# Order and engine of the state-space table preparation in a two-layer decoder trunk (GLA, then S5)

## The chip, the cores and the metric

The kernel runs on one core of one Trainium2 chip. The metric is the device time of one execution in microseconds (us), lower is better. The core's engines run their own instruction streams and wait for each other by semaphores: TensorE (PE; PEld is its weight loading), VectorE (DVE), ScalarE (ACT), GpSimd (POOL), and SyncE (SP), which here only issues DMAs. ACT and POOL issue DMAs too. An engine takes its instructions in order: one that waits holds up all behind it.

## What is computed

Two residual layers on x (512 tokens, 1024 wide), then an RMSNorm. Layer 0 is gated linear attention (4 heads, keys 128, values 512 wide), layer 1 a diagonal state-space layer (S5) with 128 groups of 16 channels and 64 complex states each. Cut to what matters:

```
x = x + gla(rmsnorm(x))                 # q,k,v,z,r = h @ w_in; o * silu(z) @ w_out
h = rmsnorm(x);  u, z = split(h @ w_in)
dt = exp(log_dt);  lam_bar = exp(lam * dt)        # complex, per group and state
b_coef = (lam_bar - 1) / lam;  b_bar = b_coef * b
states[t] = lam_bar * states[t-1] + b_bar @ u[t]
y = real(states @ c) + d_skip * u
y = gelu(y);  y = y * sigmoid(y @ w_glu + b_glu) * silu(z)
x = x + y @ w_out
```

## The kernel before

Matmul operands are split into a high and a low fp32r part, and each product is three matmuls (`three`). Weights come in units of 512 KB: SP loads a raw tile (`wraw`, two buffers, L175), ScalarE makes the high part (`whl`, L180 or L158), and the low part is made either by VectorE (L159) or by ScalarE writing the negated raw tile (L181) to which a POOL DMA adds the weights again (L182).

The S5 layer is computed in chunks of T = 8 tokens from tables that depend only on the parameters, not on x. These tables are made during the GLA layer, in the gaps of its engines. `S5Prep.small` is a generator that makes the small per-state values. Its steps are called by `tick()`: first loads, then step sizes, angles and `bcr`, `bci` (b_coef); then on POOL the powers PR, PI of lam_bar (`cmul` on POOL, with scratch tiles `ta`, `tb`) and the angle products `et` (L1139 to L1147); then the scaled `bcr`, `bci`, the scale `em2` and, by a matmul, `kap`; from these LR, LI (powers times b_coef) and `pc`, `pd` (powers times kap), all on POOL; then the stores of these values to HBM by SP (`r8d`, `kdd`, `etd`, `bcd`, 16 stores to `lpt`, 4 to `pw`), LR and LI after a transposition on TensorE; then the loads of BA, BB, rho8h and kd, where ScalarE negates half of BB (L1236). `zero()` clears the left part of the convolution buffer `kz` by 16 stores of SP.

The heavy part is a plan of steps, `prep.step(mark, code, cb)`, one for each of 16 blocks of 8 groups: F (`compute` on VectorE, `load` of the next block, storing the block before), Z (`finish_z`: convolution matrix, diagonal), E (`etab`: a table of angles from `et`), G (`gcopy`). `hook()` takes the next step from the plan after a fixed number of matmul units, from the second head of the GLA layer on. Each head runs gate, `proj_qk`, `proj_v`, the output projection of the head before, and `proj_z`, with the attention pieces (scores, state, mix) woven in. The output of a head is transposed (L399) and split (L161, L162) before its projection.

The final order on each engine is not the program's: a list scheduler simulates the engines and issues by priority, which is program order plus an offset (`later(n)`). `issue_after(ins)` keeps what is inside behind `ins` on its engine; `mark` holds the last matmul, split and weight load. Tiles come from pools of fixed size; a tile used again waits for its readers.

The scale table `etac` (16 by 8 values from `etd`) is read much later, by `uscale` in the S5 layer (L744), but its load stands on ScalarE's queue at L692 without a mark.

Of the kernel before, what the change touches and what calls it, by code (L numbers as in the profile page):

```python
# [87 lines left out]
def trunk_kernel(  # L88
# [539 lines left out]
    for h in range(NH):  # L628
# [26 lines left out]
        if h == 0:  # L655
            weave([z], tk)
            prep.zero()
            tick()
# [33 lines left out]
    A.dma_start(out=etac, in_=bass.AP(prep.etd.tensor, prep.etd.offset, [[0, 16], [NB, GB], [1, NB]]))  # L692
# [237 lines left out]
class S5Prep:  # L930
    def __init__(self, tc, dr, C_, T_, PT, ident, q4, q2, big, tmp, s_bi, s_xc):
# [12 lines left out]
        self.bcd = dr.tile([2, NS, NG], F32, name="bcd")  # L944
# [7 lines left out]
    def zero(self):  # L952
        zero = self.tmp()[:, :112]
        self.nc.gpsimd.memset(zero, 0.0)
        kzf = self.kz.bitcast(F32).rearrange("g i w -> (g i) w")
        for k in range(16):
            self.nc.sync.dma_start(out=kzf[k * P:(k + 1) * P, 0:112], in_=zero)
# [4 lines left out]
    def small(self, lam_re, lam_im, log_dt, s_d):  # L962
# [157 lines left out]
        def cmul(dr_, di_, xr, xi, yr, yi, wv):  # L1120
            u, v = ta[:, :, :wv], tb[:, :, :wv]
            tt(u, xr, yr, MUL)
            tt(v, xi, yi, MUL)
            tt(dr_, u, v, SUB)
            tt(u, xr, yi, MUL)
            tt(v, xi, yr, MUL)
            tt(di_, u, v, ADD)
# [11 lines left out]
        self.et = [self.big().rearrange("p (g c) -> p g c", c=8) for _ in range(4)]  # L1139
        for er, ei, k0 in ((self.et[2], self.et[3], 1), (self.et[0], self.et[1], 4)):  # L1140
            G.memset(er[:, :, 0:1], 1.0)
            G.memset(ei[:, :, 0:1], 0.0)
            for k in range(3):
                wv = 2 ** k
                cb_ = cosv[:, k0 + k, :].unsqueeze(2).to_broadcast([P, W, wv])
                sb_ = sinv[:, k0 + k, :].unsqueeze(2).to_broadcast([P, W, wv])
                cmul(er[:, :, wv:2 * wv], ei[:, :, wv:2 * wv], er[:, :, :wv], ei[:, :, :wv], cb_, sb_, wv)  # L1147
        dm = self.dm = C_([P, 16], "dm")
        G.tensor_copy(out=dm, in_=self.ident[:, 0:16])
        for g in range(1, GB):  # L1150
            tt(dm, dm, self.ident[:, 16 * g:16 * g + 16], ADD)
        self.par = C_([P, 2], "par")
        V.tensor_reduce(out=self.par, in_=self.ident.rearrange("p (q e i) -> p e q i", e=2, i=16), axis=AX.XY, op=ALU.add)
        V.tensor_scalar(out=self.par, in0=self.par, scalar1=2.0 ** -SS, scalar2=None, op0=MUL)
# [14 lines left out]
        vt(bci, bci, bet, MUL)  # L1169
        vt(t1, cmx, eb, MUL)  # L1170
# [21 lines left out]
             bcr.unsqueeze(2).to_broadcast([P, W, 8]), bci.unsqueeze(2).to_broadcast([P, W, 8]), 8)  # L1192
# [3 lines left out]
        tt(pc[:, :, 0, :], PR[:, :, 0:8], kb, MUL)  # L1196
        tt(pd[:, :, 1, :], PI[:, :, 0:8], kb, MUL)
        ts(pc[:, :, 1, :], pd[:, :, 1, :], -1.0, MUL)
        ts(pd[:, :, 0, :], pc[:, :, 0, :], -1.0, MUL)
        G.tensor_copy(out=pd[:, :, 1, :], in_=pc[:, :, 1, :])  # L1200
# [8 lines left out]
        for ri, b in enumerate((bcr, bci)):  # L1209
            for k in range(2):  # L1210
                nc.sync.dma_start(out=self.bcd[ri][:, k * 64:(k + 1) * 64], in_=b[k * 64:(k + 1) * 64, :])
        for ri, src in enumerate((LR, LI)):
            for q in range(2):
                pt = self.PT()
                for k in range(4):
                    PE.transpose(pt[:64, k * P:(k + 1) * P], src[:, :, 4 * q + k], self.ident)
                ev = h2k()[:64].rearrange("g (a b c) -> g a b c", a=4, b=2)
                V.tensor_copy(out=ev.rearrange("g a b c -> g (a b c)"), in_=pt[:64, :])
                for k in range(4):
                    jp = 7 - (4 * q + k)  # L1220
                    nc.sync.dma_start(out=self.lpt[jp, :, ri].rearrange("(q g) p -> g q p", q=2), in_=ev[:, k])
        for ri, src in enumerate((pc, pd)):
            for k in range(2):
                nc.sync.dma_start(out=self.pw[ri * 64:(ri + 1) * 64, k * 64:(k + 1) * 64, :].rearrange("p g t -> p (g t)"),
                                  in_=src[k * 64:(k + 1) * 64].rearrange("p g k t -> p (g k t)"))
# [193 lines left out]
```

## Time and profile before

| | us |
|---|---|
| median of 3 runs | 1041.02 (1040.5 to 1044.96) |
| profiled execution, its own time | 1047.47 |
| its span in the trace | 1045.8 |
| PE busy / share | 918.1 / 88% |
| DVE busy / share | 714.4 / 68% |
| ACT busy / share | 471.8 / 45% |
| POOL busy / share | 141.8 / 14% |

Busy shares are averages over stages with different limits. Matmuls overlap in the trace, so the pace of a stretch is read from its matmul count. "Idle before" in a timeline is the time for which the engine stood ahead of an instruction, and the name behind the arrow is what released it. The granted clock is a share of full speed.

### The profile page before, as it was taken

How to read it: one execution, taken by the hardware profiler on the slowest of the kernel's cores; microseconds unless marked ns; L12 is line 12 of the kernel's file. 1: busy time of each engine (PE TensorE's matmuls, PEld its weight loads, DVE VectorE, ACT ScalarE, POOL GpSimd, SP SyncE). 2: the span in 40 equal slices, each digit the busy share in tenths (PEclk: the TensorE clock that was granted, in tenths of full speed). 3: DMA queues.
4: the chain of work that ended last, by engine and by line, in shares of the span. 5: the costliest groups of instructions: out<-in, count | busy, mean ns of one | idle time of the engine just before them, and what ended most of it. 6: DMA issues, size and time to landing. Idle time of an engine off the chain costs nothing.

```text
span 1045.8 us, 13633 instructions
## 1 busy us (share of the span) xinstructions
PE 918.1 (88%) x5019; PEld 716.4 (69%) x5019; DVE 714.4 (68%) x1225; ACT 471.8 (45%) x707; POOL 141.8 (14%) x248
## 2 busy tenths in 40 slices
PE   6795961799979983989998979999999999999996
PEld 5573740576757762757777768787778888888885
DVE  5793459996998688887947758798998542324322
ACT  5553342554635554533666573743443532313212
POOL 3174701131112221110310000000000000000000
PEclk9997985899979996999999989999989999999998
DMA  8884466899979999798676436788756422353312
GB/s 259 230 182 93 86 188 179 250 306 276 285 225 242 287 296 288 193 306 287 228 237 186 153 100 221 243 274 256 230 155 215 132 95 86 101 161 101 101 61 80
DMA packets 116915, 205.78 MB, mean 197 GB/s; under 512 B 32401, under 2 KB 67777, under 8 KB 116849
## 3 DMA queue, kind: packets, MB, share of 16 engines
q1 hardware_dynamic: 100736, 154.68, 48.2%
q0 software_dynamic: 13152, 45.24, 16.5%
q10 hardware_dynamic: 2960, 4.99, 1.4%
q8 instruction: 39, 0.64, 0.3%
q14 instruction: 28, 0.22, 0.1%
HBM read 167.69 MB, written 45.59 MB: 204 GB/s over the span
## 4 chain that ended last, share of the span: by engine, by line
PE 55%; DMA 13%; DVE 12%; issue 9%; ACT 6%; SPq 2%; POOL 1%; ACTq 0%; POOLq 0%; DVEq 0%
PE pd L193 7%; PE pd L194 7%; PE pd L195 6%; PE pd L190 5%; PE pd L189 5%; PE pd L191 5%; ACT u L723 3%; DMA big<-s_xc 3%; DMA wraw<-w_v 2%; PE po L189 2%; PE po L190 2%; PE po L191 2%; DMA q<-s_bi 2%; PE pt L189 1%; PE pt L190 1%
## 5 line engine op out<-in xcount | busy, mean ns | idle before, releaser
L159 DVE TENSOR_TENSOR whl<-wraw,whl 128x1024 fp32r<-128x1024 f32 x100 | 122.2, 1224 | 162.9 <-ACT whl L158 161.1
L158 ACT CAST whl<-wraw 128x1024 fp32r<-128x1024 f32 x100 | 104.9, 1049 | 200.8 <-PE pd L194 59.7
L193 PE MATMUL pd<-whl,actA 128*128 128x512 f32 x384 | 153.5, 405 | 15.6 <-ACT whl L158 9.6
L194 PE MATMUL pd<-whl,actA 128*128 128x512 f32 x384 | 153.9, 401 | 0.0
L195 PE MATMUL pd<-whl,actA 128*128 128x512 f32 x384 | 151.9, 401 | 0.0
L189 PE MATMUL pd<-actA,whl 128*128 128x512 f32 x256 | 102.9, 409 | 8.8 <-ACT u L723 7.4
L191 PE MATMUL pd<-actA,whl 128*128 128x512 f32 x256 | 102.4, 401 | 0.0
L193 PEld LDWEIGHTS pd<-whl,actA 128*128 128x128 f32 x384 | 73.7, 192 | 33.6 <-ACT whl L158 9.6
L195 PEld LDWEIGHTS pd<-whl,actA 128*128 128x128 f32 x384 | 73.3, 191 | 17.7 <-issue 2.4
L194 PEld LDWEIGHTS pd<-whl,actA 128*128 128x128 f32 x384 | 73.5, 191 | 16.2 <-issue 0.8
L193 PE MATMUL pd<-whl,q 128*128 128x512 f32 x192 | 78.8, 411 | 5.2 <-DVE tmp L387 4.9
L194 PE MATMUL pd<-whl,q 128*128 128x512 f32 x192 | 78.4, 408 | 0.0
L189 PEld LDWEIGHTS pd<-actA,whl 128*128 128x128 f32 x256 | 49.2, 192 | 21.3 <-ACT u L723 8.3
L180 ACT CAST whl<-wraw 128x1024 fp32r<-128x1024 f32 x36 | 37.7, 1047 | 57.0 <-PE pd L194 31.6
L191 PEld LDWEIGHTS pd<-actA,whl 128*128 128x128 f32 x256 | 49.1, 192 | 11.4
L189 PE MATMUL po<-actA,whl 128*128 128x512 f32 x128 | 51.4, 402 | 3.0 <-ACT whl L180 3.0
L190 PE MATMUL pd<-actA,whl 128*128 128x512 f32 x128 | 52.0, 406 | 0.0
L191 PE MATMUL po<-actA,whl 128*128 128x512 f32 x128 | 50.3, 395 | 1.5 <-DMA whl<-w_qk 1.5
L195 PE MATMUL pd<-whl,q 128*128 128x512 f32 x128 | 51.5, 412 | 0.0
L723 ACT ACTIVATE u<-pd,rsP 64x256 f32<-64x256 f32 x64 | 47.9, 748 | 3.1 <-DVE rsP L690 2.2
L190 PE MATMUL pd<-big,whl 128*128 128x512 f32 x120 | 48.6, 407 | 0.6 <-DVE big L159 0.6
L193 PEld LDWEIGHTS pd<-whl,q 128*128 128x128 f32 x192 | 37.4, 195 | 16.2 <-DVE tmp L387 5.3
(331 smaller groups left out, 2035.6 us busy)
## 6 DMA issues: line engine op xcount, KB each, us to landing
wraw<-w_glu SPq DMA_DIRECT2D x32, 512.0 KB, 3.5
wraw<-w_v SPq DMA_DIRECT2D x16, 512.0 KB, 4.5
wraw<-w_z SPq DMA_DIRECT2D x16, 512.0 KB, 5.8
whl<-w_z POOLq DMA_DIRECT2D x16, 512.0 KB, 9.2
q<-lpt SPq DMA_DIRECT2D x16, 512.0 KB, 5.7
q<-s_bi SPq DMA_DIRECT2D x16, 512.0 KB, 7.6
wraw<-w_out SPq DMA_DIRECT2D x16, 512.0 KB, 7.7
bmd<-q POOLq DMA_DIRECT2D x16, 512.0 KB, 6.9
```

Of the source, the lines that this page charges most:

```text
L158: i0 = A.copy(out=dst_hi, in_=src)
L159: i1 = V.tensor_tensor(out=dst_lo, in0=src, in1=f(dst_hi), op=SUB)
L180: A.copy(out=hi, in_=raw)
L189: PE.matmul(acc, lhsT=wh, rhs=ah, start=first, stop=False)
L190: PE.matmul(acc, lhsT=wh, rhs=al, start=False, stop=False)
L191: mark["pe"] = PE.matmul(acc, lhsT=wl, rhs=ah, start=False, stop=last).ins
L193: PE.matmul(acc, lhsT=ah, rhs=wh, start=first, stop=False)
L194: PE.matmul(acc, lhsT=ah, rhs=wl, start=False, stop=False)
L195: mark["pe"] = PE.matmul(acc, lhsT=al, rhs=wh, start=False, stop=last).ins
L723: A.activation(out=dst, in_=src, func=AF.Copy, scale=rsP[hs, tb:tb + 1])
```

## The change

Seven edits. (1) `bcd` holds a third table, the negated `bci`, and the lower half of BB is loaded from it; ScalarE's negation is gone. (2) LR, LI, `pc` go from POOL to VectorE, `pd` to ScalarE, and the angle products `et` (still on POOL) and `dm`, `par` are made after the stores in the program. (3) The 16 stores to `lpt` become 4, the transposes being taken in reverse order. (4) The load of `etac` is issued by SP, behind the weight load last marked. (5) `zero()` is one POOL store instead of 16 SP stores. (6) The first block's load is a step "L" of its own, between the last `tick()` of the first head and `zero()`; the F step of block 0 no longer issues it. (7) The diagonal is added by one instruction instead of two.

```diff
         if h == 0:
             weave([z], tk)
+            tick()
+            prep.step(mark, "L", 0)
             prep.zero()
-            tick()
...
-    A.dma_start(out=etac, in_=bass.AP(prep.etd.tensor, prep.etd.offset, [[0, 16], [NB, GB], [1, NB]]))
+    with tc.issue_after(mark["sp"]):
+        S.dma_start(out=etac, in_=bass.AP(prep.etd.tensor, prep.etd.offset, [[0, 16], [NB, GB], [1, NB]]))
...
-        kzf = self.kz.bitcast(F32).rearrange("g i w -> (g i) w")
-        for k in range(16):
-            self.nc.sync.dma_start(out=kzf[k * P:(k + 1) * P, 0:112], in_=zero)
+        kzf = self.kz.bitcast(F32).rearrange("g i w -> (g i) w").rearrange("(k p) w -> p k w", p=P)
+        self.nc.gpsimd.dma_start(out=kzf[:, :, 0:112], in_=zero.unsqueeze(1).to_broadcast([P, 16, 112]))
...
-        def cmul(dr_, di_, xr, xi, yr, yi, wv):
+        def cmul(dr_, di_, xr, xi, yr, yi, wv, E=G):
...
-        self.et = [self.big().rearrange("p (g c) -> p g c", c=8) for _ in range(4)]
...   (the whole block L1139 to L1154, et, dm, par, moves behind the stores)
+        nbi = t64()
+        vs(nbi, bci, -1.0, MUL)
...
         cmul(LR, LI, PR[:, :, 1:9], PI[:, :, 1:9],
-             bcr.unsqueeze(2).to_broadcast([P, W, 8]), bci.unsqueeze(2).to_broadcast([P, W, 8]), 8)
+             bcr.unsqueeze(2).to_broadcast([P, W, 8]), bci.unsqueeze(2).to_broadcast([P, W, 8]), 8, V)
...
-        tt(pc[:, :, 0, :], PR[:, :, 0:8], kb, MUL)
-        tt(pd[:, :, 1, :], PI[:, :, 0:8], kb, MUL)
-        ts(pc[:, :, 1, :], pd[:, :, 1, :], -1.0, MUL)
-        ts(pd[:, :, 0, :], pc[:, :, 0, :], -1.0, MUL)
-        G.tensor_copy(out=pd[:, :, 1, :], in_=pc[:, :, 1, :])
+        vt(pc[:, :, 0, :], PR[:, :, 0:8], kb, MUL)
+        stt(pc[:, :, 1, :], PI[:, :, 0:8], -1.0, kb, MUL, MUL)
+        A.activation(out=pd[:, :, 0, :], in_=pc[:, :, 0, :], func=AF.Copy, scale=-1.0)
+        A.copy(out=pd[:, :, 1, :], in_=pc[:, :, 1, :])
...
-        for ri, b in enumerate((bcr, bci)):
+        for ri, b in enumerate((bcr, bci, nbi)):
...
-                for k in range(4):
-                    jp = 7 - (4 * q + k)
-                    nc.sync.dma_start(out=self.lpt[jp, :, ri].rearrange("(q g) p -> g q p", q=2), in_=ev[:, k])
+                nc.sync.dma_start(out=self.lpt[4 - 4 * q:8 - 4 * q, :, ri].rearrange("j (q g) p -> g j q p", q=2), in_=ev)
...
-            nc.sync.dma_start(out=self.BB[hs], in_=self.bcd[1])
+            nc.sync.dma_start(out=self.BB[hs], in_=self.bcd[2 - k])
...
-        A.activation(out=self.BB[0:64], in_=self.BB[0:64], func=AF.Copy, scale=-1.0)
...
-        dk = self.C2([P, 16], "dk")
-        V.tensor_tensor(out=dk, in0=self.dm, in1=self.kd[:, cb:cb + 1].to_broadcast([P, 16]), op=MUL)
-        V.tensor_tensor(out=ke[:, 0:16], in0=ke[:, 0:16], in1=dk, op=ADD)
+        V.scalar_tensor_tensor(out=ke[:, 0:16], in0=self.dm, scalar=self.kd[:, cb:cb + 1], in1=ke[:, 0:16],
+                               op0=MUL, op1=ADD)
...
-                else:
-                    self.load(0)
...
+            elif code == "L":
+                self.load(cb)
```

## Rows read from the trace of the kernel before

**Rows 1.** The page: busy tenths of TensorE in 40 equal slices of the span.
```profile
PE   6795961799979983989998979999999999999996
```

**Rows 2.** Busy time by stretch: length; PE, PEld, DVE, ACT, POOL (count); granted clock; DMA share; GB/s.
```profile
84.00:107.00 23.00, 10.24 (x34) 6.73 (x33) 10.37 (x23) 9.73 (x18) 11.92 (x20) 0.71 0.50 106
...
104.00:144.00 40.00, 40.00 (x179) 31.63 (x178) 21.05 (x38) 17.14 (x30) 20.68 (x24) 0.96 0.47 103
146.00:192.00 46.00, 8.67 (x29) 4.96 (x30) 38.51 (x70) 12.24 (x21) 6.00 (x11) 0.53 0.76 233
192.00:440.00 248.00, 217.67 (x958) 165.93 (x957) 210.17 (x389) 128.86 (x196) 47.45 (x70) 0.92 0.92 262
```

**Rows 3.** Timeline of TensorE: start, duration, instruction, [idle before it <- releaser].
```profile
86.70 0.51 PE L193 MATMUL po<-big,big 128*128 128x512 f32 x1 [1.72 <-ACT big L502]
...
102.36 0.79 PE L193 MATMUL po<-big,big 128*128 128x512 f32 x1 [8.98 <-ACT big L520]
...
154.86 1.11 PE L399 MATMUL pt<-ident,big 128*128 128x128 f32 x4 [9.48 <-DVE q L162]
...
173.65 0.80 PE L484 MATMUL pt<-big,big 128*128 128x128 f32 x2 [14.20 <-DVE big L159]
```

**Rows 4.** Timeline of ScalarE.
```profile
83.87 0.31 ACT L1236 ACTIVATE BB<-BB 64x128 f32<-64x128 f32 x1 [6.46 <-DMA BB<-bcd]
...
100.78 1.06 ACT L181 ACTIVATE whl<-wraw 128x1024 fp32r<-128x1024 f32 x1 [11.19 <-DMA etd<-tmp]
```

**Rows 5.** Timeline of VectorE.
```profile
101.75 0.18 DVE L1331 TENSOR_TENSOR dk<-dm,kd 128x16 f32<-128x16 f32 x1 [9.38 <-DMA kd<-kdd]
...
153.32 1.23 DVE L1283 TENSOR_TENSOR q<-q,q 128x1024 f32<-128x1024 f32 x1 [7.61 <-DMA q<-s_bi]
```

**Rows 6.** Timeline of SP: start and duration of runs of DMA issues.
```profile
101.86 0.35 SPq L175 DMA_DIRECT2D wraw<-w_v  x1
117.98 2.99 SPq L957 DMA_DIRECT2D kz<-tmp  x6
122.12 12.66 SPq L1221 DMA_DIRECT2D lpt<-q  x16
134.88 2.92 SPq L1224 DMA_DIRECT2D pw<-q  x4
137.85 6.87 SPq L957 DMA_DIRECT2D kz<-tmp  x10
...
146.76 0.85 SPq L175 DMA_DIRECT2D wraw<-w_out  x2
...
527.73 0.53 SPq L1340 DMA_DIRECT2D gmd<-kz  x1
```

**Rows 7.** POOL's groups by shape: count; busy, mean ns; idle before, releasers.
```profile
L1259 POOL DMA_DIRECT2D tab<-q x32 | 17.1, 541 | 39.1 <-DVE q L1256 38.9 <-issue 0.2
...
L1335 POOL DMA_DIRECT2D kz<-kf x16 | 9.3, 580 | 60.9 <-DVE kf L1334 38.8 <-DVE big L168 15.6 <-DVE big L167 4.3
...
L984 POOL TENSOR_TENSOR q<-q,big 128x512 f32<-128x512 f32 x6 | 7.3, 1230 | 0.1
```

**Rows 8.** VectorE's groups by shape.
```profile
L1283 DVE TENSOR_TENSOR q<-q,q 128x1024 f32<-128x1024 f32 x16 | 19.5, 1220 | 18.4 <-DMA q<-s_bi 18.2 <-DMA cmd<-q 0.2
...
L1284 DVE TENSOR_TENSOR q<-q 128x512 f32<-128x512 f32 x16 | 10.9, 683 | 2.1 <-DMA cmd<-q 2.1
...
L999 DVE TENSOR_TENSOR big<-big 128x64 f32<-128x64 f32 x13 | 5.0, 393 | 0.1
...
L1331 DVE TENSOR_TENSOR dk<-dm,kd 128x16 f32<-128x16 f32 x16 | 2.7, 169 | 9.4 <-DMA kd<-kdd 9.4
...
L999 DVE TENSOR_TENSOR big<-big,q 128x64 f32<-128x64 f32 x4 | 0.8, 220 | 0.0
```

**Rows 9.** The page: DMA issues, KB each, median us from issue to landing.
```profile
wraw<-w_v SPq DMA_DIRECT2D x16, 512.0 KB, 4.5
...
whl<-w_v POOLq DMA_DIRECT2D x12, 512.0 KB, 8.1
```

More of the change, by code (lines that the diff above doesn't have):

```diff
@@ L943, in __init__ @@
         self.lpt = dr.tile([T, NG, 2, NS], F32, name="lpt")
-        self.bcd = dr.tile([2, NS, NG], F32, name="bcd")
+        self.bcd = dr.tile([3, NS, NG], F32, name="bcd")
         self.r8d = dr.tile([NS, NG], F32, name="r8d")
@@ L1118, in small @@
         ta, tb = t8(), t8()
-        def cmul(dr_, di_, xr, xi, yr, yi, wv):
+        def cmul(dr_, di_, xr, xi, yr, yi, wv, E=G):
             u, v = ta[:, :, :wv], tb[:, :, :wv]
[L1122 to L1127, printed above, removed]
+            tt(u, xr, yr, MUL, E)
+            tt(v, xi, yi, MUL, E)
+            tt(dr_, u, v, SUB, E)
+            tt(u, xr, yi, MUL, E)
+            tt(v, xi, yr, MUL, E)
+            tt(di_, u, v, ADD, E)
         G.memset(PR[:, :, 0:1], 1.0)
@@ L1137, in small @@
             cmul(PR[:, :, base:base + w], PI[:, :, base:base + w], PR[:, :, 1:1 + w], PI[:, :, 1:1 + w], yr, yi, w)
-        self.et = [self.big().rearrange("p (g c) -> p g c", c=8) for _ in range(4)]
[L1140 to L1154, printed above, removed]
         yield
@@ L1215, in small @@
                 for k in range(4):
-                    PE.transpose(pt[:64, k * P:(k + 1) * P], src[:, :, 4 * q + k], self.ident)
+                    PE.transpose(pt[:64, k * P:(k + 1) * P], src[:, :, 4 * q + 3 - k], self.ident)
                 ev = h2k()[:64].rearrange("g (a b c) -> g a b c", a=4, b=2)
                 V.tensor_copy(out=ev.rearrange("g a b c -> g (a b c)"), in_=pt[:64, :])
-                for k in range(4):
-                    jp = 7 - (4 * q + k)
-                    nc.sync.dma_start(out=self.lpt[jp, :, ri].rearrange("(q g) p -> g q p", q=2), in_=ev[:, k])
+                nc.sync.dma_start(out=self.lpt[4 - 4 * q:8 - 4 * q, :, ri].rearrange("j (q g) p -> g j q p", q=2), in_=ev)
         for ri, src in enumerate((pc, pd)):
@@ L1225, in small @@
                                   in_=src[k * 64:(k + 1) * 64].rearrange("p g k t -> p (g k t)"))
+        self.et = [self.big().rearrange("p (g c) -> p g c", c=8) for _ in range(4)]
+        for er, ei, k0 in ((self.et[2], self.et[3], 1), (self.et[0], self.et[1], 4)):
+            G.memset(er[:, :, 0:1], 1.0)
+            G.memset(ei[:, :, 0:1], 0.0)
+            for k in range(3):
+                wv = 2 ** k
+                cb_ = cosv[:, k0 + k, :].unsqueeze(2).to_broadcast([P, W, wv])
+                sb_ = sinv[:, k0 + k, :].unsqueeze(2).to_broadcast([P, W, wv])
+                cmul(er[:, :, wv:2 * wv], ei[:, :, wv:2 * wv], er[:, :, :wv], ei[:, :, :wv], cb_, sb_, wv)
+        dm = self.dm = C_([P, 16], "dm")
+        G.tensor_copy(out=dm, in_=self.ident[:, 0:16])
+        for g in range(1, GB):
+            tt(dm, dm, self.ident[:, 16 * g:16 * g + 16], ADD)
+        self.par = C_([P, 2], "par")
+        V.tensor_reduce(out=self.par, in_=self.ident.rearrange("p (q e i) -> p e q i", e=2, i=16), axis=AX.XY, op=ALU.add)
+        V.tensor_scalar(out=self.par, in0=self.par, scalar1=2.0 ** -SS, scalar2=None, op0=MUL)
         yield
```

## The prediction

> **What bounds the kernel now.** I read the slices of the page first. TensorE is at 9 tenths or more in most of them; the low ones lie in the first half: slices 4, 6, 7 and 8 (78 to 209 us), which hold what the change touches, and slice 16, which it does not [rows 1]. The end of the kernel is matmuls in a row, so what can be won lies where TensorE stands. The table of stretches sizes it. Between 104 and 144 us TensorE never rests: 179 matmuls in 40.00 us, 0.223 us each. Between 84 and 107 us it does only 34, worth 34 x 0.223 = 7.6 us at that pace, in 23 us: 15.4 us lost, 12.8 of them standing and 2.6 by a granted clock of 0.71. Between 146 and 192 us it does 29, worth 6.5 us, in 46 us: 39.5 us lost, with the clock at 0.53, close to the lower of its two levels (1.2 of 2.4 GHz) [rows 2]. The two holes, 55 us together, are the cap on any gain. The view of TensorE's waits and the same view of the engines it waits for say why.
>
> Hole one: attention waits 1.72 us and then 8.98 us for ScalarE [rows 3]. ScalarE stands 6.46 us at L1236 (the sign of BB, which needs the BB load) and 11.19 us behind the load of the scale table, which waits for its store of etd to land [rows 4]. In that second stretch VectorE stands too: 9.38 us at L1331, whose operand kd is still on its way [rows 5]. The two cover each other, so only removing both frees the time.
>
> Hole two: TensorE waits 9.48 us for VectorE's splits of the transposed head output, then 14.20 us for VectorE again [rows 3]. The first is not VectorE's work: it stands 7.61 us at L1283 for the s_bi load of block 0 [rows 5]. That load was late because SP issues in order and had 6 zero stores, 16 lpt stores (12.66 us), 4 pw stores (2.92) and 10 zero stores (6.87) ahead of it; the first w_out weights went out only at 146.76 us [rows 6]. From 153.32 us on VectorE is the bound: 38.51 us of 46 busy, all but those 7.61, while from 104 to 144 us it was busy for 21.05 of 40 [rows 2].
>
> **The change, part by part.** *BB, scale table, diagonal (hole one).* BB's sign is made by one small VectorE product (at most 0.39 us by the 128x64 rows [rows 8]) and two more bcd stores; ScalarE's 6.46 us wait goes. The scale table is queued on SP behind the last weight load of the GLA layer, hundreds of us later, when etd is long in memory; it costs SP one issue, and nobody behind it waits, since the first reader is the S5 scaling; without that cover it would cost a landing, of the order of a weight load's 4.5 us [rows 9]. The diagonal no longer needs a tile that can run ahead and wait on kd: its instruction now also needs the convolution matrix, so VectorE cannot meet it until finish_z. Available: 1.72 + 8.98 us of waits and 2.6 us of clock = 13.3 us.
>
> Against it stand new VectorE instructions in the same stretch: LR and LI, six of 128x512 at 0.683 us = 4.1 us, pc twice 0.683 = 1.4 us, nbi 0.2: 5.7 us [rows 8]. VectorE has 10.37 us of work in these 23 us [rows 2]; with all 5.7 inside, the stretch cannot fall below 16.1 us and the gain is 6.9. With none on attention's path it is 13.3. VectorE stands for 12.6 of the 23 us, more than it is given, so I take the middle, 10. The copies that make pd go to ScalarE, busy for 9.73 of the 23 us; without that slack they would cost some 0.7 us each, the size of such a product.
>
> POOL took 7.3 us for six of these products [rows 7]. The same product of 128x64 took VectorE 0.393 us on average in one group, where POOL was multiplying beside it in part, and 0.220 in another [rows 8]; were that ratio of 1.79 to hold for LR and LI, 4.1 us would be 7.3, the gain 3.2 lower. The Trainium skill, "SBUF — State Buffer", Who interferes with whom, says that a VectorE instruction with two SBUF inputs and a GpSimd instruction that reads SBUF exclude each other. By it POOL's neighbours set that ratio. Here POOL's angle products use the same scratch tiles ta and tb, so they cannot start before LI is done; I keep 4.1. POOL's products end later for it, but it loses more work than LR and LI take, and their first reader is etab, a step behind compute(0).
>
> *SP's queue (hole two).* The 16 lpt stores become 4. A store of 0.79 us with four times the rows costs 4 x 0.79 = 3.2 us at most; SP's issue of gmd, whose rows are many and short as well, took 0.53 us [rows 6], so the four cost 2.1 to 3.2 us and about 10 us leave SP. The 16 zero stores leave SP altogether: 2.99 + 6.87 = 9.9 us. Both together are 20 us ahead of the first load. Besides, stores and load(0) no longer wait for POOL to finish the angle products: they can go right behind LR, LI and pc. Block 0 is then in SBUF well before 145 us, and the 7.61 us stand with the 9.48 us of TensorE behind it goes; the w_out loads at 146.76 us move forward as much. Bounds 7.6 and 9.5; I take 9.
>
> *VectorE's backlog.* With block 0 there, VectorE can do compute(0) in its 19 free microseconds before 144: three of 1.22, four of 0.683 and some small ones, 7.2 us, and two etabs, 12 x 0.683 = 8.2 us [rows 2, 8]. At most 15.4 us leave the bound stretch; none, if the list scheduler leaves them behind attention. The load is freed but the steps keep their place, so I take about half, 7. The clock comes back with the matmuls and is counted in the first hole only.
>
> *Diagonal, rest.* 16 instructions of 0.169 us = 2.7 us [rows 8], of which perhaps 1 lies where VectorE bounds.
>
> *Zero on POOL.* One POOL store takes the place of 16 issues of SP. POOL's issues take 0.541 us for a 64-row store and 0.580 for a 128-row store [rows 7]: 0.04 us per 64 rows would make 2048 rows 1.8 us; 16 stores in one would be 9.3 us. Behind it in POOL's order wait the accumulating weight loads (L182) of the next v projection, so this can reach TensorE. Lower end nothing, as POOL loses more than 7.3 us of products ahead of those loads; I take 2. The Trainium skill, "DMA: Bandwidth & Descriptors", Issuing engine by pattern, puts a simple store on SP and calls that path generally the faster; by it this part would be a loss, and no row here shows a POOL store of 2048 rows.
>
> *After 192 us* up to 440 us TensorE is busy for 217.67 of 248 us, VectorE for 210.17, with the DMA engines at 0.92 [rows 2]. The S5 steps are tied to matmuls, so the gain should be carried along; for closer demand on VectorE and DMA I take off 3.
>
> Sum: 10 + 9 + 7 + 1 - 2 - 3 = 22 us. The profiled execution took 1047.47 us (span 1045.8), 6.4 above the median of 1041.02, so 22 us off it is 1025.5, and off the median 1019.
>
> **Rivals.** *More comes free (chance 0.15).* Nothing of the new VectorE work is on the path, and the whole backlog moves: 13.3 + 9.5 + 15.4 + 1 - 2 = 37 us, 1004. For it: 19 free microseconds on VectorE. Against: the DMA engines at 0.92 from 192 us on.
>
> *The queue only moves to POOL (0.14).* The zero store holds POOL for 9.3 us ahead of L182, and the next v projection waits for it: 22 + 2 - 9.3 = 15 us gained, 1026. The page named for that store speaks for it; against it stands that 64 rows more cost 0.04 us.
>
> *No change (0.11).* Attention's own chain and the new 5.7 us fill hole one (6.9 us won), and VectorE's order fills hole two again: the 7.6 us are used by S5 steps, not by attention, and the later stretches, VectorE-bound, take back what came: 6.9 - 2 - 3 = 2 us and up to 3 more from hole two, 1036 to 1039. For it: VectorE is the bound for 38 us as it stands; against: this bound has 19 idle microseconds right ahead.
>
> *Slower (0.09): SP held by the early load.* load(0) is traced ahead of the next layers' weights; its lp read needs the lpt stores landed, these the transposes on TensorE, these LR and LI. If the scheduler keeps the transposes where they are now, SP stands there from about 102 to 135 us, with the last w_v load, now issued at 101.86 us [rows 6], behind it. From raw to usable takes 4.5 us of landing, about 2 of ScalarE and 8.1 of accumulation [rows 9], some 15 us with the issues: 150, while the last quarter of the projection, 24 matmuls before 144 us and so from about 138 on, would start near 138 - 10 = 128. 22 us lost, with hole one's 10 won, hole two shrunk by no more than 5 and 3 for POOL: about 10 slower, 1051. It decides from the point where that load goes out later than 113 us (128 - 15). Against it: with ScalarE and VectorE no longer standing, LR and kap can be ready before 100 us (an estimate).
>
> **How the numbers follow.** The likeliest case, 22 us with its terms between their inner bounds (1010 to 1028), has 0.51. Below 1001 I leave 0.07, above 1040 0.12; so the range is 1001 to 1040. A half per cent, 5.2 us, is about what a measurement here can tell from no change. Faster than 1035.8: 0.51 + 0.15 + 0.14 = 0.80; same 0.11; slower 0.09.
>
> **What would show it.** In the changed profile ScalarE has no wait of 6 us or more between 75 and 105 us, and VectorE none for kd; proj_qk of the second head starts near 97 us instead of 107; SP issues the first lp load before 120 us; VectorE does compute(0) before 140 us; the hole with the clock near 0.5 shrinks from 46 to some 30 us. I am wrong if POOL's store lasts longer than about 5 us with weights behind it, if SP stands at lpt with a weight load behind it, or if the second hole stays as long as it is, with VectorE full.

## The result and the profile after

The changed kernel takes 1029.58 us (median of 4 executions, 1025.89 to 1032.04) against 1042.99 for the kernel before: ratio 0.9871, 95% interval 0.9839 to 0.9902, some 13.4 us less. One of the four executions behind 1042.99 took 1822.03 us; without it the median is 1041.02, the base of the forecast, and the gain 11.4 us. In 78 more executions of the kernel before, beside the experiments, the medians were 1042.16 to 1043.53, so I keep 13.4. I had forecast 1019 with a range of 1001 to 1040. Faster was right; the size was 22 forecast against 13.4.

The profiled executions differ by 17.95 us (1047.47 and 1029.52), because the one of before lies 4.5 us above its own median. To see where they lie apart I count weight matmuls: each trace has 3408 of them (L189 to L195, or those lines shifted by an edit), in nearly the same order, so the time at which the n-th starts is a milestone. This table is worked out from the starts in each trace; the columns after the first are lengths in us between the matmuls named. "Hole two" is 433rd to 481st. The runs' names are explained below. The ratios are to the kernel before as it was executed beside each run, not quotients of the medians in this column.

```
              median us    ratio [95%]               profiled  289th  289th  hole  481st    1105th   2257th
                                                               at     -433rd two   -1105th  -2257th  -end
before        1042.99                                 1047.47  105.1  38.7   57.1  178.6    375.9    290.4
after         1029.58      0.9871 [0.9839, 0.9902]    1029.52   93.8  39.1   53.4  179.1    374.0    288.5
e1            1046.51      1.0043 [1.0023, 1.0063]    1047.71  108.4  38.8   55.6  177.1    375.4    290.4
e2            1043.37      1.0002 [0.998, 1.0024]     1036.55   92.1  39.3   48.2  188.5    378.9    287.8
e10           1049.40      1.0041 [1.0014, 1.0067]    1047.45  105.7  39.7   50.2  183.6    378.4    288.1
e6            1048.73      1.0044 [1.0022, 1.0066]    1049.55  106.1  37.8   62.2  179.4    373.8    288.5
e3            1032.80      0.9902 [0.9869, 0.9935]    1033.98   91.8  43.3   50.2  176.9    381.6    288.3
e4            1039.88      0.9964 [0.9943, 0.9986]    1038.49   95.9  40.5   54.4  177.1    380.7    287.8
e7            1036.93      0.9946 [0.9922, 0.997]     1034.18   96.0  37.5   50.9  177.5    377.0    293.5
e8            1042.48      0.9971 [0.994, 1.0001]     1038.58   95.5  38.4   51.9  181.8    376.0    293.1
e5            1029.53      0.9867 [0.9833, 0.99]      1028.79   93.6  37.6   44.5  188.2    373.8    289.1
e11           1031.71      0.9899 [0.9871, 0.9926]    1035.12   97.9  39.3   42.5  182.5    383.1    288.2
e9            1037.03      0.9964 [0.993, 0.9997]     1033.88   93.0  38.2   54.0  179.9    371.8    294.9
e12           1045.79      1.0036 [1.001, 1.0061]     1047.20  105.9  37.9   55.6  174.2    382.9    289.1
```

In the two first rows: hole one closed (11 us at the 433rd matmul, 143.8 to 132.9), hole two 3.7 us shorter, the rest 3.2 us shorter (844.8 to 841.6 from the 481st matmul to the end). These three make up the 17.95 us of the profiled executions; in which of them the 4.5 us lie that the medians do not show, no trace tells.

The page after, TensorE in 40 slices; beside [rows 1] slice 4 (78 to 105 us there) is full and the low slices are now 6 and 7:

```profile
PE   6899933999799987979899799999899999999996
```

Stretches after, with the columns of [rows 2]:

```profile
84.00:107.00 23.00, 20.79 (x82) 15.90 (x81) 8.30 (x20) 10.68 (x20) 6.82 (x17) 0.85 0.69 166
104.00:144.00 40.00, 30.41 (x140) 23.93 (x138) 27.35 (x47) 17.91 (x28) 24.25 (x36) 0.93 0.73 182
133.00:174.00 41.00, 8.20 (x32) 4.58 (x30) 37.00 (x66) 12.41 (x25) 5.49 (x10) 0.56 0.66 194
...
192.00:440.00 248.00, 227.95 (x981) 167.80 (x980) 211.33 (x374) 129.45 (x201) 51.03 (x69) 0.94 0.94 274
```

From 84 to 107 us TensorE does 82 matmuls instead of 34. From 133 to 174 us it does 32 in 41 us at a granted clock of 0.56: hole two has moved some 11 us ahead, with VectorE at 37.00 of 41 us. TensorE's waits after, those of [rows 3] in both holes:

```profile
88.40 0.50 PE L193 MATMUL po<-big,big 128*128 128x512 f32 x1 [0.56 <-DVE big L506]
91.03 0.80 PE L193 MATMUL po<-big,big 128*128 128x512 f32 x1 [1.66 <-ACT big L520]
...
148.45 1.12 PE L399 MATMUL pt<-ident,big 128*128 128x128 f32 x4 [14.04 <-DVE q L162]
...
158.16 0.79 PE L484 MATMUL pt<-big,big 128*128 128x128 f32 x2 [6.39 <-DVE big L159]
166.69 0.79 PE L484 MATMUL pt<-big,big 128*128 128x128 f32 x2 [7.51 <-DVE q L162]
...
174.91 0.80 PE L193 MATMUL pd<-whl,q 128*128 128x512 f32 x1 [4.05 <-DVE big L162]
```

The 8.98 us behind ScalarE are gone. Every wait in the second hole is now for VectorE. SP after, beside [rows 6]:

```profile
104.53 0.38 SPq L1272 DMA_DIRECT2D big<-s_xc  x1
105.00 1.31 SPq L1205 DMA_DIRECT2D lpt<-q  x2
108.01 0.33 SPq L175 DMA_DIRECT2D wraw<-w_out  x1
114.24 1.94 SPq L1205 DMA_DIRECT2D lpt<-q  x2
116.28 1.63 SPq L175 DMA_DIRECT2D wraw<-w_out  x1
126.95 0.57 SPq L1267 DMA_DIRECT2D q<-lpt  x1
127.57 1.51 SPq L1269 DMA_DIRECT2D q<-s_bi  x1
129.18 1.71 SPq L175 DMA_DIRECT2D wraw<-w_out  x2
```

The four `lpt` stores take 3.25 us of issue in all (16 took 12.66), and the first w_out load goes out at 108 us. But SP stands from 118 to 127 us in front of block 0's load. It needs the last `lpt` store, and that landed late: issued at 114.88 us, landed at 126.88, 12.00 us on its way. Beside it were the zero store (0.9 MB, issued by POOL at 113.64, landed 9.89 us later), an accumulating w_v load (11.08) and a raw w_out load (11.84). POOL's own row of that store:

```profile
113.64 1.54 POOL L958 DMA_DIRECT2D kz<-tmp  x1
```

VectorE begins compute(0) at 135.04 us, after it stood idle for 19.6 of the 39.1 us from the 289th to the 433rd matmul.

### The profile page after: what moved, and what is told of

Read it like the earlier page. It is cut to its first block, busy times and chain, and to the rows that moved or that the text cites. A ratio compares the mean times of both kernels' runs of the same rounds, so it can differ in the third digit from the quotient of the medians.

```text
span 1027.8 us, 13590 instructions
## 1 busy us (share of the span) xinstructions
PE 923.6 (90%) x5019; PEld 716.6 (70%) x5019; DVE 714.2 (69%) x1218; ACT 472.0 (46%) x708; POOL 138.7 (13%) x238
## 4 chain that ended last, share of the span: by engine, by line
PE 61%; DMA 10%; DVE 10%; ACT 8%; issue 8%; POOL 2%; SPq 1%; POOLq 0%; ACTq 0%; DVEq 0%
PE pd L193 8%; PE pd L195 8%; PE pd L194 8%; PE pd L190 5%; PE pd L189 5%; PE pd L191 5%; ACT u L725 4%; PE po L189 2%; PE po L190 2%; PE po L191 2%; DMA q<-s_bi 2%; PE po L194 1%; PE pt L189 1%; PE pt L190 1%; PE po L195 1%
## 5 line engine op out<-in xcount | busy, mean ns | idle before, releaser
L195 PE MATMUL pd<-whl,actA 128*128 128x512 f32 x384 | 150.8, 398 | 0.0
L189 PE MATMUL pd<-actA,whl 128*128 128x512 f32 x256 | 102.5, 407 | 7.7 <-ACT u L725 5.9
L193 PEld LDWEIGHTS pd<-whl,actA 128*128 128x128 f32 x384 | 72.9, 190 | 31.9 <-ACT whl L158 9.2
L194 PEld LDWEIGHTS pd<-whl,actA 128*128 128x128 f32 x384 | 72.9, 190 | 17.7 <-DMA whl<-w_v 1.5
L195 PEld LDWEIGHTS pd<-whl,actA 128*128 128x128 f32 x384 | 72.5, 189 | 16.4 <-issue 1.2
L189 PEld LDWEIGHTS pd<-actA,whl 128*128 128x128 f32 x256 | 48.7, 191 | 20.2 <-ACT u L725 6.9
L191 PEld LDWEIGHTS pd<-actA,whl 128*128 128x128 f32 x256 | 48.8, 191 | 11.3
L189 PE MATMUL po<-actA,whl 128*128 128x512 f32 x128 | 51.9, 405 | 3.9 <-ACT whl L180 3.9
L195 PE MATMUL pd<-whl,q 128*128 128x512 f32 x128 | 52.2, 418 | 0.5 <-DVE q L162 0.5
```

Source lines behind the costliest of these rows:

```text
L189: PE.matmul(acc, lhsT=wh, rhs=ah, start=first, stop=False)
L191: mark["pe"] = PE.matmul(acc, lhsT=wl, rhs=ah, start=False, stop=last).ins
L193: PE.matmul(acc, lhsT=ah, rhs=wh, start=first, stop=False)
L194: PE.matmul(acc, lhsT=ah, rhs=wl, start=False, stop=False)
L195: mark["pe"] = PE.matmul(acc, lhsT=al, rhs=wh, start=False, stop=last).ins
```

## The experiments

In the expectations "theory" is mine at that time, and it changed.

**e1: the scale table alone.** Kernel before with one edit:

```diff
-    A.dma_start(out=etac, ...)
+    with tc.issue_after(mark["sp"]):
+        S.dma_start(out=etac, ...)
```

> The kernel before with the scale table's load moved to SP and nothing else. Cover theory: VectorE still stands for kd at the diagonal's first product until about 100 us, so attention resumes no more than 3 us earlier and the 289th weight matmul starts at 102 to 105 us (105.1 before); total 0 to 3 us less. Rival, ScalarE alone sets the first hole: the 289th starts at 96 to 98 us and the total falls by 7 to 9 us.

Not faster (ratio 1.0043), and the 289th matmul starts at 108.4 us, so both expectations of that place failed. ScalarE's wait for the table is gone, and VectorE stands in its place:

```profile
104.44 0.23 DVE L1332 TENSOR_TENSOR dk<-dm,kd 128x16 f32<-128x16 f32 x1 [11.03 <-DMA kd<-kdd]
```

So the two stalls did cover each other, as the prediction had it.

**e2: all three parts for hole one** on the kernel before: e1's edit, the diagonal in one instruction, BB stored negated.

> The kernel before with the three edits of the first hole: scale table's load on SP, diagonal in one instruction, BB stored negated. Theory that these three close the first hole and the rest of the change gives little: the 289th weight matmul starts at 93 to 96 us, the second hole (from the 433rd to the 481st weight matmul, 57.1 us before, 53.3 after the change) stays at 55 to 59 us, and the total falls by 8 to 12 us. Rival, the moved products and stores are needed for it too: the 289th starts after 99 us and the total falls by less than 5 us.

The hole closes (289th matmul at 92.1 us, 13 earlier; the theory had 93 to 96). Hole two is shorter too, which it had not, and in the profile TensorE leads by 21.3 us at the 481st matmul. The time is that of the kernel before: 1.0002. The profiled execution is the fastest of ten, 6.8 us below their median, so it overstates the lead that lasts; but even in it half of the lead is gone by the 1105th matmul. One place is visible, and most of the loss lies there: the lead is 21.6 us at the 745th matmul (248 us) and 13.4 at the 769th (262 us). TensorE waits 5.77 us for a w_v half, whose raw load was 14.08 us on its way (issued 233.11, landed 247.20) and whose accumulation took another 9.75.

```profile
257.07 0.77 PE L194 MATMUL pd<-whl,actA 128*128 128x512 f32 x1 [5.77 <-DMA whl<-w_v]
```

**e10: the other half**, all that e2 leaves out: powers on VectorE ahead of the angle products, 4 `lpt` stores, zero on POOL, the load step.

> The kernel before with the other half of the change: the powers and their stores ahead of the angle products and on VectorE and ScalarE, 4 stores to lpt, zero() as one POOL store, the load step; the scale table's load stays on ScalarE, BB's sign stays on ScalarE and the diagonal stays two instructions with a tile of its own. Theory (the two halves need each other, since the second hole's parts can only be used when attention comes early): the 289th weight matmul at 105 us or later, as before, the second hole shorter by at most 4 us, and the time 0 to 5 us faster than before. Rival (these parts carry the gain alone): 9 to 14 us faster, ratio 0.987 to 0.991.

Ratio 1.0041: about 4 us slower. Hole two is 7 us shorter, hole one stays (105.7 us). In the total neither half is worth anything by itself; together they are worth 13.4 us. That much of the theory held; its 0 to 5 us faster did not.

**e3: the zero store ahead of the weave**, on the changed kernel (`prep.zero()` before `weave([z], tk)`), so that its 0.9 MB do not travel beside the `lpt` stores.

> The changed kernel with the one POOL zero store ahead of the first head's z projection instead of behind it. Theory that its burst of short pieces holds the DMA engines: the last lpt store lands within 6 us (12.0 now), the first lp load goes out before 121 us (126.95 now), the second hole shrinks from 53.3 to 47 us or less, total 5 to 8 us below the changed kernel. Rival, the second hole is VectorE's own queue of work, whenever the load comes: the load is earlier, the hole stays at 51 to 55 us, total within 3 us of the changed kernel.

The last `lpt` store lands in 2.72 us and block 0's load goes out at 118.95 us, 8 earlier. Hole two is 50.2 us long instead of 53.4, the stretch ahead of it 4.2 longer, and the time is not below that of the changed kernel. So the burst theory was right on the landing and the load and wrong on the hole and the time. The late landing was real; removing it gained nothing.

**e5: two etab steps later.** The changed kernel, with these lines behind the making of the plan ("N" does nothing):

```diff
+    plan = [("N", 0) if s in (("E", 0), ("E", 1)) else s for s in plan]
+    plan.insert(plan.index(("Z", 9)) + 1, ("E", 0))
+    plan.insert(plan.index(("Z", 11)) + 1, ("E", 1))
```

> The changed kernel, with only the place of two steps of the plan moved: the etab steps of blocks 0 and 1 (12 VectorE products each block pair row, some 4 us of VectorE each) stand behind finish_z of blocks 9 and 11 instead of ahead of the first blocks; nothing is left out. Theory (the second hole lasts as long as VectorE's queue of S5 steps ahead of attention's splits is long): with two etabs less in that queue the hole, 433rd to 481st weight matmul, goes from 53.3 us to 45 (43 to 47) and the median lies 5 to 8 us below the changed kernel's, ratio to the kernel before 0.980 to 0.983. Rival (the late first load of lp sets the hole, VectorE's queue only fills it): the hole stays at 51 us or more and the time stays within 3 us of the changed kernel. Third outcome: the hole shrinks but VectorE's work comes back later between 200 and 440 us, the hole near 45 and the total within 3 us.

The hole shrinks to 44.5 us: VectorE's queue sets its length, not the load. The time does not move (1029.53), which is the third outcome that I had named, though by another cause than VectorE's work: from the 481st to the 1105th matmul it loses 9.1 us again. A large part of the loss is found in the trace. An etab is not only VectorE's 4.1 us, but also four POOL stores of 256 KB. Here is SP, then ScalarE, where they now fall:

```profile
330.63 2.79 SPq L175 DMA_DIRECT2D wraw<-w_v  x2
333.52 2.13 SPq L1270 DMA_DIRECT2D q<-lpt  x1
...
349.21 0.33 SPq L175 DMA_DIRECT2D wraw<-w_v  x1
```

```profile
347.18 1.04 ACT L180 CAST whl<-wraw 128x1024 fp32r<-128x1024 f32 x1 [14.46 <-DMA wraw<-w_v]
...
349.09 0.35 ACT L1330 ACTIVATE tmp<-pt,par 128x128 f32<-128x128 f32 x1
```

The second raw w_v load of that pair took 16.32 us to land, behind the four stores at 329.33 to 330.95 us. ScalarE stands 14.46 us for the raw weights ahead of it, with a conversion of S5 (L1330) behind it, for which VectorE then stands 11.49 us, and TensorE 5.78 us for VectorE's L392. The lead over the changed kernel is 8.1 us at the 1057th matmul (344 us) and 1.5 at the 1081st (358 us). That the four stores made this load late is not shown: in the changed kernel, without them there, two w_v loads of the same stretch took 13.37 and 15.31 us (issued at 341.76 and 346.30).

**e11: the same two steps first.** The changed kernel, with the angle products ahead of LR and LI, scratch of their own for LR and LI, and

```diff
+    plan = [("E", 0), ("E", 1)] + [s for s in plan if s not in (("E", 0), ("E", 1))]
```

> The changed kernel with nothing left out, and the angle products put back ahead of LR and LI on POOL, LR and LI getting scratch tiles of their own so that neither waits for the other, and the two etab steps of blocks 0 and 1 put first in the plan, so that VectorE can do them in the 27 us in which it stands between 104 and 133 us. Theory (VectorE's S5 work bounds the stretch from 133 to 500 us, so that work moved within it comes back, as in the run with the etabs behind blocks 9 and 11, and only work moved ahead of it counts): the second hole at most 47 us, and the time 5 to 9 us below the changed kernel, ratio 0.978 to 0.982. Rival (what bounds the stretch up to 500 us is not VectorE's sum, but each step's own loads and stores): the hole shrinks, and the time stays within 3 us of the changed kernel.

The etabs run at 126 us, the hole is 42.5 us long, the shortest of all, and the time is 1031.71. Part is paid ahead of the hole: the 289th matmul starts 4.1 us later. POOL now multiplies beside LR, LI and attention's splits from 74 to 98 us, and VectorE's instructions are longer for it. VectorE's groups by shape from 74 to 100 us (count, busy us, mean ns), of the changed kernel and then of e11 (its lines are one higher for `tt`):

```profile
L985 DVE TENSOR_TENSOR q<-q,big 128x512 f32<-128x512 f32 x4 | 2.6, 686 | 0.0
L170 DVE TENSOR_SCALAR big<-big,ges 128x512 fp32r<-128x512 f32 x3 | 1.4, 479 | 0.0
...
L168 DVE TENSOR_TENSOR big<-att,big 128x128 fp32r<-128x128 f32 x4 | 1.1, 284 | 0.0
L167 DVE CAST big<-att 128x128 fp32r<-128x128 f32 x4 | 0.8, 223 | 0.0
```

```profile
L986 DVE TENSOR_TENSOR q<-q,big 128x512 f32<-128x512 f32 x4 | 3.6, 927 | 0.0
L168 DVE TENSOR_TENSOR big<-att,big 128x128 fp32r<-128x128 f32 x4 | 2.2, 564 | 0.0
L170 DVE TENSOR_SCALAR big<-big,ges 128x512 fp32r<-128x512 f32 x3 | 2.1, 708 | 0.0
...
L167 DVE CAST big<-att 128x128 fp32r<-128x128 f32 x4 | 1.8, 470 | 0.0
```

The rest comes back between 229 and 290 us, where ScalarE waits 5.96 and 3.27 us for raw w_v loads. That VectorE's sum bounds the stretch up to 500 us therefore fell: the work was moved ahead of it, and the gain still did not last.

**e4 and e6: the zero store back on SP, and alone on POOL.** e4 is the changed kernel with the 16 SP stores; e6 is the kernel before with the one POOL store.

```diff
-        for k in range(16):
-            self.nc.sync.dma_start(out=kzf[k * P:(k + 1) * P, 0:112], in_=zero)
+        self.nc.gpsimd.dma_start(out=kzf[:, :, 0:112], in_=zero.unsqueeze(1).to_broadcast([P, 16, 112]))
```

> The changed kernel with the 16 zero stores back on SP. Burst theory: they go out one by one between the other stores, the last lpt store lands within 6 us, but the w_out weights behind them on SP come 4 to 8 us later, so the second hole is 50 to 56 us and the total within 3 us of the changed kernel. SP queue theory of the prediction: w_out's second raw load later than 120 us and the total 5 to 10 us above the changed kernel. VectorE queue theory: hole 51 to 55 us, total within 3 us.

> The kernel before, with one edit of the seven: zero() is one POOL store of 2048 rows instead of 16 stores of SP. Theory A (SP's 16 zero stores cost some 10 us by themselves, because the first lp load and the third and fourth w_out loads stand behind them): 5 to 10 us faster than before, ratio 0.990 to 0.995, and the last first-layer output weights load before 140 us instead of at 146.76. Theory B (they cost only once the other waits of that stretch are gone, since SP stands for the lpt stores anyway): within 3 us of the kernel before, ratio 0.997 to 1.003. My prediction's own price for this edit, a loss of 2 us, would give 1.002.

Undone, it costs 10 us; done alone, it costs 5 (1.0044), more than any of the three expectations of e6 had it. In e6 the four w_out loads go out at 118.60, 133.55, 143.63 and 146.59 us; in the kernel before the first two go out at 146.76 and 147.24 and the last at 161.95. (The expectation took 146.76 for the last.) There SP stood 15.8 us for the zeros that POOL had to make first (L954), ahead of the first zero store at 117.98 us, a wait that the prediction does not have. So the move did free SP, as theory A had it, but not block 0's load, which goes out at 144.37 us (144.76 before) behind the `lpt` stores, and earlier w_out loads alone gained nothing. In e4 w_out's second raw load goes out at 130.07 us and the time is 10 us up, both as the SP queue theory had it; yet in its profile only 1 of the 9 us is in hole two, where that theory sees the loss; 3.5 lie before it, 6.7 between the 1105th and the 2257th matmul, and over 2 come back elsewhere.

**e7: no load step; e8: powers back on POOL**, each on the changed kernel.

```diff
-            prep.step(mark, "L", 0)
...
+                else:
+                    self.load(0)
```

```diff
-             bcr.unsqueeze(2).to_broadcast([P, W, 8]), bci.unsqueeze(2).to_broadcast([P, W, 8]), 8, V)
+             bcr.unsqueeze(2).to_broadcast([P, W, 8]), bci.unsqueeze(2).to_broadcast([P, W, 8]), 8)
...   (pc, pd on POOL too, and the angle products ahead of them)
```

> The changed kernel, with the first block's load put back into the F step of block 0 instead of a step of its own between the last tick of the first head and zero(). Theory (the load waits for the landing of the last lpt store at 126.9 us wherever it stands in the program, and so the step does nothing): the load's issue within 2 us of 127, the hole 53 +- 2 us, the time within 3 us of the changed kernel (ratio to before 0.984 to 0.990). Rival (the step of its own lets the load go ahead of the next weights): the load issued 5 us or more later and the time 5 to 9 us above the changed kernel.

> The changed kernel, with edit 2 undone: the angle products stand on POOL ahead of LR, LI, pc and pd, which POOL makes too; the other six edits stay. Theory (the stores of the powers set when block 0 is in SBUF): the lpt and pw stores go out 8 us or more later, the first lp load at 135 us or later, the second hole starts and ends later, 5 to 10 us above the changed kernel (ratio to before 0.992 to 0.997). Rival (VectorE's 5.7 us of new work cost attention as much as the earlier stores give): within 3 us of the changed kernel or below it.

By the medians e7 loses 7.4 us and e8 12.9. By the profiles neither loses anything where the edit is: block 0's load goes out at 124.37 and 128.58 us (126.95 in the changed kernel), hole two is 50.9 and 51.9 us long, and at the 481st matmul both are level with the changed kernel (184.5 and 185.9 against 186.2). Some 5 us of each loss lie some 550 us later, behind the 2257th matmul (293 us to the end instead of 288.5), and e8 loses another 5 between 186 and 740 us. e7's theory fell on the time and nearly held on the place (the load's issue 2.6 us and the hole 2.1 us off, where it had allowed 2); e8's fell on the place, and its loss is above the expected 5 to 10 us by the medians and at the edge by the ratio (0.9971).

**e9 and e12: the order alone.** No edit, only priority offsets of the list scheduler:

```diff
-LOWS = {'F': 30, 'Z': 30, 'E': 100, 'G': 0}
+LOWS = {'F': 31, 'Z': 31, 'E': 101, 'G': 0}    (e9, on the changed kernel)
+LOWS = {'F': 36, 'Z': 36, 'E': 100, 'G': 0}    (e12, on the kernel before)
```

> The changed kernel with all its work and all its edits, and one constant moved by one: the priority offsets of the S5 steps F, Z and E are 31, 31 and 101 instead of 30, 30 and 100. The first instructions that change places are the third block's on VectorE, behind the second hole (after about 230 us); up to there the two are the same. Theory (the order that the list scheduler happens to find is worth some us by itself, and the 7 us between the changed kernel and the one without the load step are at least in part this): the time differs from the changed kernel's by 3 us or more in either direction. Rival (neighbouring swaps even out, and single edits can be read to 2 us): within 2 us of the changed kernel, ratio 0.985 to 0.989.

> The kernel before with none of the seven edits and all its work: the priority offsets of the steps F and Z are 36 instead of 30. The order is the same up to VectorE's 691st instruction (past 400 us) and differs in hundreds of places behind it, the stretch from 739 to 762 us among them, where the changed kernel with an offset moved by one lost what it lost. Theory (order alone moves the kernel before as much as it moved the changed one): the time differs from 1043 by 3 us or more, in either direction; if it is slower, the segment from the 2257th weight matmul to the end takes 293 us or more instead of 290.4. Rival (only the changed kernel was lucky or unlucky, the order of the kernel before is worth nothing): within 2 us of 1043, ratio 0.998 to 1.002.

e9 is 7.4 us slower than the changed kernel by the medians (interval 0.993 to 0.9997 against 0.9839 to 0.9902), e12 some 3.6 us slower than the kernel before (1.0036). In e9's profile nearly all is level or ahead up to 737 us (2.5 us ahead there); then, in the S5 layer, it falls 6.7 us behind, and ends 4 behind. e7 and e8 lose some 5 us at the same place. The stretches of e9, then of the changed kernel:

```profile
740.00:745.00 5.00, 2.39 (x26) 1.46 (x25) 4.94 (x7) 4.20 (x8) 0.00 (x0) 0.64 0.96 350
745.00:750.00 5.00, 3.31 (x8) 2.39 (x9) 5.00 (x9) 3.34 (x6) 0.00 (x0) 0.50 1.01 319
```

```profile
740.00:745.00 5.00, 3.12 (x7) 2.01 (x7) 4.94 (x9) 5.00 (x11) 0.00 (x0) 0.74 0.89 259
745.00:750.00 5.00, 5.00 (x21) 3.98 (x21) 5.00 (x10) 3.08 (x5) 0.00 (x0) 0.92 0.93 333
```

VectorE is full in both. In e9 it does other work before the gate's product, for which TensorE stands 3.41 us, and the granted clock is at 0.50:

```profile
746.69 0.79 PE L189 MATMUL pd<-actA,whl 128*128 128x512 f32 x1 [3.41 <-DVE tmp L750]
```

In e12 that place is undisturbed (289.1 us to the end) and the loss by the medians has no single place: the profiles end together. So the theory of e9 and e12 held for the size (for e12 by the median; its interval begins at 1 us), and its place for e12 did not.

## Why the prediction was right, and where its sizes were wrong

**Hole one: right, by the mechanism named.** Forecast 10 us, found 11. ScalarE's waits for BB and the table are gone (its longest between 75 and 105 us, 6.04, is for TensorE's own result, though by its length it breaks the sign that I had named), so is VectorE's for kd, and the 289th matmul starts 11.3 us earlier. e1 and e2 show the cover: one wait removed gives nothing, all removed give 13 us at that place. In all fourteen traces the 289th matmul starts at 92 to 98 us where the three parts are in, and at 105 us or later where they are not. The new VectorE work (5.7 us) cost little: e2, without it, is there only 1.7 us earlier. LR and LI took 6 x 0.687 = 4.1 us, as I had kept it, because POOL multiplied nothing beside them: from 75 to 91 us it stood 4.38 and 10.19 us for ScalarE at the accumulating loads (L182), with the angle products behind. Whether the shared scratch tiles would have held them too, as I had argued, this trace cannot show. With scratch of their own and the angle products first (e11) LR and LI took 5.6 us. The Trainium skill, "SBUF — State Buffer", Who interferes with whom, whose rule I had weighed there, agrees with e11: two-input products lengthen from 0.686 to 0.927 us, and so do the casts (0.223 to 0.470), which by that page can use the shared pair of ports as well. An instruction with one of its inputs in PSUM stays as it was (L506, one line higher in e11: 0.746 and 0.740 us):

```profile
L506 DVE SCALAR_TENSOR_TENSOR big<-po,ges,tmp 128x512 f32<-128x512 f32 x2 | 1.5, 746 | 1.4 <-ACT tmp L505 1.4
```

```profile
L507 DVE SCALAR_TENSOR_TENSOR big<-po,ges,tmp 128x512 f32<-128x512 f32 x2 | 1.5, 740 | 0.0
```

**Hole two: the failed step.** The terms 9 (SP's queue), 7 (VectorE's backlog), 1 and -2 came to 15 us; the hole shrank by 3.7. Hole two before and after, with the columns of [rows 2]:

```profile
143.85:200.94 57.09, 19.15 (x73) 13.09 (x71) 49.28 (x90) 18.56 (x33) 7.08 (x13) 0.61 0.72 215
```

```profile
132.87:186.25 53.38, 19.67 (x73) 13.80 (x71) 49.38 (x89) 16.01 (x32) 6.57 (x12) 0.62 0.62 180
```

VectorE is busy for 49.28 us before and 49.38 after. So the backlog, of which I took half to move by itself into the idle time, did not move at all: the term 7 came to nothing. What the hole lost is idle time of VectorE, 7.8 us before and 4.0 after: the 7.61 us for block 0's load are gone, but waits of 2.79 us for a later s_bi load and 0.96 us have come, and so the term 9 came to 3.8.

SP's issue was sized rightly (four stores of 3.25 us, at the upper bound of 2.1 to 3.2; zero off SP), but block 0's load does not go out when SP is free: it waited for a store to land, and went out at 126.95 us instead of before 120. Where that was mended (e3, load at 118.95 us), the hole gave only 3 us more: with the load there, VectorE still has compute(0), two etabs, compute(1) and the splits of attention behind one another, from 127 us on. e5 and e11 took the etabs out of the hole by hand and got 9 to 11 us there, more than the 7 that I had counted, and nothing in the total. Of the signs that I had named, the first lp load before 120 us and the hole of some 30 us did not come; compute(0) before 140 us did.

**Carrying to the end: small, as forecast, but wrong in its nature.** I took off 3 us. The profiles show the rest 3.2 us shorter; if the 4.5 us by which the profiled execution of before is slow lie there, it is 1.3 us longer. But a lead does not simply last. e5 led the changed kernel by 10.6 us at the 481st matmul and by 1.1 at the end, e2 led the kernel before by 21.3 and by 10.9 in the profiles, and by nothing in the medians. From the 481st to the 1105th matmul these four kernels do the same 729 matmuls:

```profile
186.25:365.34 179.09, 169.23 (x729) 124.93 (x727) 154.29 (x271) 100.27 (x150) 43.01 (x56) 0.96 0.94 275
```

```profile
175.67:363.85 188.18, 172.17 (x729) 127.33 (x727) 153.14 (x270) 98.93 (x147) 38.17 (x55) 0.93 0.92 261
```

```profile
200.94:379.50 178.56, 165.81 (x729) 126.01 (x728) 149.78 (x270) 97.16 (x144) 37.35 (x54) 0.95 0.95 272
```

```profile
179.65:368.17 188.52, 168.37 (x729) 125.55 (x727) 159.92 (x275) 98.08 (x144) 41.67 (x58) 0.95 0.92 266
```

These are the changed kernel, e5, the kernel before and e2. Times the rate they move 49.2, 49.1, 48.6 and 50.1 MB, with the DMA engines busy for 0.92 to 0.95 of the stretch, and most of the lead was lost at raw weights that took 14 and 16 us to land: 8.2 us of it in e2 and 6.6 in e5. e11 lost 5.4 us (6.7 at the 697th matmul, 1.3 at the 721st) where ScalarE stood for raw w_v. I read this as a stretch that is limited by transfers, so that whoever comes early waits there. The waits are shown; the limit is argued, and one thing speaks against it: the two kernels that come early move their bytes more slowly (261 and 266 GB/s) than the others, and e12 moved its 48.6 MB in 174.20 us, at 279. No run took traffic out of that stretch.

In e2 VectorE also put work off: it is busy for 37.56 us in hole two, as the line below shows, instead of 49.28, and for 159.92 us behind it instead of 149.78. That cost little by then: TensorE's wait of 6.42 us for VectorE at 277.59 us has its like in the kernel before (5.77 us at 291.22 us), and from the 769th to the 817th matmul around it the lead falls by 1.6 us.

```profile
131.40:179.65 48.25, 19.54 (x72) 13.48 (x71) 37.56 (x75) 16.81 (x31) 5.44 (x10) 0.65 0.76 215
```

**Zero on POOL: the issue was right, the sign is open.** 1.54 us of POOL (I had worked out 1.8), and the rival in which it holds POOL for 9.3 us fell. The Trainium skill, "DMA: Bandwidth & Descriptors", Issuing engine by pattern, gives a simple store to SP; e6, where the move alone costs 5 us, goes its way, e4, where undoing it costs 10, goes against it. Neither difference lies at the store, and neither is far above what order alone does (e9, e12).

**The rivals.** *More comes free* (1004) needed the backlog to move. *The queue only moves to POOL* (1026) came nearest in time, by another cause than its own. *No change* had the mechanism that I gave too little weight: VectorE's order filled hole two again. *Slower* had SP standing at block 0's load; it stood there for 9 us, with two w_out loads behind it, and not with a w_v load behind it as that rival needed.

**What stays open.** How much of the 13.4 us is the edits. One priority offset moved by one costs the changed kernel 7.4 us by the medians (9.7 by the ratios); so the 7 to 13 us that single edits seem to be worth (e4, e7, e8) are not far above what order alone does, and lie in good part hundreds of us behind them. With the order of e9 the same seven edits came out at 1037, near the end of the range at 1040: that the time lies well inside it is in part luck. The changed kernel was executed four times, most variants ten. Firm is the sign: the changed kernel and six of its seven variants have a ratio below 1 with the whole interval (the seventh, e8, reaches 1.0001), and no kernel with half of the change or less has. Why executions of one kernel spread by up to 14 us (e9: 1032.59 to 1046.79) no trace here tells, as one execution of each was profiled. No variant beat the changed kernel beyond the interval.

## What to carry to other kernels

Where two engines stand at the same time, remove both waits: here one alone gave nothing at that place (e1), and both gave 13 us there (e2). But read the total too: e2's 13 us did not reach the end, and neither half of the change was faster by itself. Ask of a hole not only which load is late, but what the bounding engine's order puts into it once the load is there, and what stretch comes next: here a lead of 10 us was worth 1 us or nothing ahead of 180 us in which raw weights land late, with the DMA engines busy for 0.92 to 0.95. In a kernel whose order is found by a list scheduler, measure the scatter that a meaningless change of order brings before reading an edit's worth: here it was 4 to 7 us.

## What the runs showed of the hardware

The zero store slowed the transfers beside it. It (2048 rows of 448 bytes, 0.9 MB) took POOL 1.54 us to issue and 9.89 us to land. Of the two 128 KB `lpt` stores issued behind it one took 5.20 us and the other 12.00; with the zero store moved away (e3) they took 2.61 and 2.72, and the w_out load behind them 3.74 instead of 11.84. It was on POOL's queue and these on SP's. Whether its bytes or its short rows do this no run separates. The Trainium skill, "Trainium Kernel Development and Optimization", Key Constraints, says that DMAs of all issuing engines run on the same 16 DMA engines and that another queue saves issue time only; these rows agree.

A raw w_v load of 512 KB took 3.3 to 4.1 us in the kernel before when issued between 68 and 102 us, where the DMA engines are busy for some half of the time (0.50 from 84 to 107 us, [rows 2]), and 16.24 us when issued at 231 us, where they are busy for 0.92. The 14 us in e2 and 16.3 us in e5 are no more than that.
